# Staged weight forms, stores on another queue and moved cache copies in a hybrid decoder layer

## The chip, the cores and the metric

The kernel runs on one core of a Trainium2 chip. The metric is device time in microseconds (us) for one execution of the whole program, the median over several runs. A change of under 0.2% (about 4 us here) can't be told from none.

## The reference, cut to what matters

One decoder layer is computed for 1024 prompt positions and 8 single-token samples (1032 columns), D_MODEL 1024, all in float32:

```python
h = _rms_norm(x, g_mix_pre)
q, k, v, c_b, u, g_a, g_c = _project(h, w_in)      # u = c_c * c_h; w_in is 1024 x 9728
o, lse = ...                                       # attention in 3 head groups, dilations 1, 4, 16
kv_s = concatenate([cache, new k and v])[-n_past:] # cache rows moved by one
a = attn @ w_attn_o
c = (c_b * causal_conv(u, conv_w)) @ w_conv_o
mix = (sigmoid(g_a) * a + sigmoid(g_c) * c) @ w_o
x = x + _rms_norm(mix, g_mix_post)
x = x + _rms_norm(square(relu(_rms_norm(x, g_ffn_pre) @ w_ff1)) @ w_ff2, g_ffn_post)
```

The samples read caches of 128, 512 and 1024 rows; those caches, moved by one row, are outputs too, copied from DRAM to DRAM.

## The kernel before

Activations lie feature-major: 128 partitions by 1032 columns per feature tile. To keep float32 accuracy TensorE multiplies two rounded parts: every operand is a pair hi + lo, and each product is three matmuls (hi·hi, lo·hi, hi·lo). A weight tile of 128x512 arrives from DRAM as `wr` (issued on SP's queue, L169), `split` makes `wh` with a copy on ScalarE (L177) and `wl` with a subtraction on VectorE or GpSimd (L178). The pool holds five such pairs in the middle of the program (seven from the attention output projection on).

The program goes through these stages:

1. Norm, then per head the q, k, v projections beside the attention (to about 620 us). At the end of each of the eight heads `copy_piece(2)` issues two cache copies of up to 1 MB, of 57 in all, on ScalarE's queue (L334).
2. `tsums` (L965): sums of halves of h for a 2x2 Strassen-Winograd scheme: VectorE and GpSimd make T1, T2, T3, T4 in two halves (j = 0, 2), each split into hi and lo. Beside them TensorE does two plain gate tiles (`gate_raw`).
3. 17 *pairs* of weight columns. `strassen` (L1001) computes two 128-column results from seven products p0 to p6 of 24 matmuls each, accumulated in PSUM tiles A, B, C in the order B A C B A B C. The evictions are done by ScalarE and VectorE: after p1 `A` is copied (L1018) and `B` is added to it (L1019); only then may p3 write `B` again. The seven weight forms of a pair are sums of its four `wr` tiles (`s1`, `s2` and others), four of them made on GpSimd by `combine` (L133). "u" pairs give conv_C and conv_h (their product goes into E, then a three-tap convolution makes y, L1086 to L1089); "y" pairs give conv_B, multiplied with y (L1066); "g" pairs give gates. y and g results are stored to DRAM (`cv_d`, `g_d`) on GpSimd's queue (L1067). 15 pairs run in a pool `cw`, beside the samples' attention (`sample_steps`, advanced in two of five half products: loads `kt`, `qb` on SP's queue, products on GpSimd, sums on VectorE), and two gate pairs in a pool `pre`, beside the scaling and splitting of the attention output (`split_heads`: DMAs for `num` and `rden`, product L1119). After each pair of the 15 `copy_piece(2)` issues two more copies, after the last two pairs four.
4. The attention output projection "wao" with the gates as multipliers (`gr` from `g_d`, sigmoid L1167, product L1171, stored as `m2_d`); the conv output is loaded and split. Then "wco", "wo", and the squared-ReLU MLP ("wf1", "wf2").

The weights' work is issued ahead: `tick()` runs once per half product; if the form's raw tiles were requested two ticks ago and a `wh`/`wl` pair is free, `split_next` issues for the next form the GpSimd sum, the ScalarE copy and the VectorE subtraction at once. Each engine runs its instructions in order, so whatever stands behind such an instruction waits with it. `pin` keeps instructions in the order of the program; a scheduler places the others.

Of the kernel before, what the change touches and what calls it, by code (L numbers as in the profile page):

```python
# [13 lines left out]
OP = mybir.AluOpType  # L14
# [23 lines left out]
def tile_decoder_layer(  # L38
# [63 lines left out]
    todo = [(64, 65), (66, 67), (70, 71), (72, 73), (74, 75)]  # L102
# [6 lines left out]
    gate_pairs = todo  # L109
# [62 lines left out]
    def split(raw, space, eng, pin_):  # L172
# [5 lines left out]
        pin_(eng.tensor_tensor(lo, raw, hi.bitcast(F32), op=OP.subtract))  # L178
        return hi, lo, space

    def split_next():
# [4 lines left out]
        ready.append((key, split(form(rs), space, lo_eng[turn[0] % len(lo_eng)], lo_pin[0])))  # L186
        for j in free:
            raws.pop((plan_key, keys[j]))[2][2] += 1
# [5 lines left out]
    def tick():  # L194
        clock[0] += 1
        if forms and max(e[2] for e in spaces) > 0 and loaded(2):
            split_next()
        fetch()

    def take(key):  # L200
        while not ready:
            if loaded(0):
                split_next()
# [140 lines left out]
    with ExitStack() as st:  # L344
# [388 lines left out]
        for h in range(8):  # L733
# [24 lines left out]
            copy_piece(2)  # L758
# [194 lines left out]
    with tc.tile_pool(name="tsum", bufs=1) as ts:  # L953
# [5 lines left out]
        def tsums(j):  # L959
            js, ks = slice(j, j + 2), slice(4 + j, 6 + j)  # L960

            def new(name, bufs=1):
                return ts.tile([P, 2, HT], F32, name=name, bufs=bufs)

            def parts(eng, n, t):  # L965
                nc.scalar.copy(TS[n][0][:, js], t)
                eng.tensor_tensor(TS[n][1][:, js], t, f32(TS[n][0][:, js]), op=OP.subtract)
            b12, b22, T2, T3, T4 = new("b12", 2), new("b22", 2), new("T2", 2), new("T3"), new("T4")
            V, G, S = nc.vector.tensor_tensor, nc.gpsimd.tensor_tensor, OP.subtract
            V(b12, f32(hh[:, js, t2]), f32(hl[:, js, t2]), op=OP.add)  # L970
# [12 lines left out]
            yield  # L983
# [5 lines left out]
        for j in (0, 2):  # L989
            for _ in tsums(j):  # L990
                run(g, 2)
# [43 lines left out]
    with ExitStack() as st:  # L1035
# [15 lines left out]

        def drive(g):
# [8 lines left out]
        def stores(D, dst, ys=None):  # L1061
            def after(p):
                if p in DONE:
# [3 lines left out]
                    nc.gpsimd.dma_start(dst[a][:, t], D[a][:, t])  # L1067
            return after
        i, ys = 0, []
        for kind, *pair in pairs:  # L1070
            D1 = cw.tile([P, T], F32, name="D1")
            if kind == "u":
                E = cw.tile([P, 2 + T], F32, name="E", bufs=2)
                nc.gpsimd.memset(E[:, 0:2], 0.0)
                u = E[:, 2:]

# [4 lines left out]
                drive(strassen(pair, (D1, u), after))  # L1081
# [10 lines left out]
            else:  # L1092
                D = D1, cw.tile([P, T], F32, name="D2")
# [4 lines left out]
            copy_piece(2)  # L1098
# [6 lines left out]
    with tc.tile_pool(name="apool", bufs=1) as apool:  # L1105
        ah = apool.tile([P, 4, T], F32R, name="ah")
        al = apool.tile([P, 4, T], F32R, name="al")
        with tc.tile_pool(name="pre", bufs=1) as pre:
            def split_heads():
                for n in range(4):  # L1110
# [5 lines left out]
                    yield  # L1116
                    yield
                    yield
# [12 lines left out]
            for pair in gate_pairs:  # L1131
# [3 lines left out]
                for _ in strassen(pair, D, stores(D, [g_d[m - 60] for m in pair])):  # L1135
                    run(heads, 1)
            run(heads)
            copy_piece(4)
# [6 lines left out]
        with tc.tile_pool(name="cpool", bufs=1) as cpool:  # L1145
# [3 lines left out]
            with tc.tile_pool(name="sga", bufs=1) as sga:  # L1149
                cvs, grs = [], []  # L1150
# [13 lines left out]
                for i in range(KT):  # L1164
                    load_gate()
                    load_cv()
                    nc.scalar.activation(grs[i], grs[i], AF.Sigmoid)  # L1167
# [13 lines left out]
                    copy_piece(1)  # L1181
# [3 lines left out]
            with tc.tile_pool(name="sgc", bufs=1) as sgc:  # L1185
# [10 lines left out]
                for _ in range(3):  # L1196
                    load()
                nc.scalar.activation(got[0][0], got[0][0], AF.Sigmoid)
                for i in range(KT):
# [11 lines left out]
                    copy_piece(1)  # L1211
# [319 lines left out]
```

## Time and profile before

| | us |
|---|---|
| median of three runs (2123.06 to 2126.0) | 2124.21 |
| profiled execution | 2112.52 |
| its span (first to last instruction) | 2110.3 |
| TensorE busy in the span | 1971.2 (93%) |
| VectorE / ScalarE / GpSimd busy | 1236.2 / 733.1 / 601.2 |

The profiled execution is one run on its own and 11.7 us shorter than the median; sums over the profile are made against 2112.5. A busy TensorE isn't always at full speed: the granted clock is given beside it (1.00 is full). "Idle before ... <- X" names what ended an idle time.

### The profile page before, as it was taken

To read this page: it belongs to the slowest core of one execution; us is meant where nothing else is said; L and a number is where in the kernel's file an instruction comes from. 1 tells how busy PE (TensorE), PEld (TensorE's weight loads), DVE (VectorE), ACT (ScalarE), POOL (GpSimd) and SP (SyncE) were. 2 spreads that over 40 slices of the span, in tenths; PEclk is the share of its full clock that TensorE was granted. 3 is DMA by queue.
4 is the path that set the end of the run, shared out by engine and by line. 5 is a ranking of instruction groups with operands and counts; after the bars stand their busy time and mean duration, and the time that the engine had idled before them with its cause. 6 is when DMAs were issued, how large, how long until landed. Compare 5 with 4: busy or idle time off the path is not lost.

```text
span 2110.3 us, 33274 instructions
## 1 busy us (share of the span) xinstructions
PE 1971.2 (93%) x13253; PEld 1945.9 (92%) x13253; DVE 1236.2 (59%) x2081; ACT 733.1 (35%) x1448; POOL 601.2 (28%) x523
## 2 busy tenths in 40 slices
PE   7999999999996889888976999999999999999997
PEld 6999999999995889888976999999999999999996
DVE  7678777787646667485553441644554554444546
ACT  4355544554433213222233334453222221222233
POOL 3233332333237444444130223211111110101113
PEclk8999999999997889999988999999999999999998
DMA  4212122313231574554569542311111111111112
GB/s 141 57 64 77 50 72 66 103 43 98 91 115 61 197 248 168 201 178 158 186 190 374 184 133 78 94 51 40 51 40 51 51 43 49 51 41 50 51 31 81
DMA packets 84459, 216.74 MB, mean 103 GB/s; under 512 B 12000, under 2 KB 22368, under 8 KB 83408
## 3 DMA queue, kind: packets, MB, share of 16 engines
q1 hardware_dynamic: 65280, 112.77, 16.7%
q10 hardware_dynamic: 8112, 68.78, 9.4%
q0 software_dynamic: 10912, 33.06, 4.9%
q8 instruction: 104, 1.70, 0.3%
q14 instruction: 51, 0.42, 0.1%
HBM read 184.17 MB, written 84.86 MB: 127 GB/s over the span
## 4 chain that ended last, share of the span: by engine, by line
PE 48%; DVE 6%; DMA 6%; issue 4%; POOL 2%; ACT 1%; SPq 0%; ACTq 0%; DVEq 0%; POOLq 0%
PE ps_mm L218 14%; PE ps_mm L222 14%; PE ps_mm L221 14%; DVE wl L178 2%; DMA qb<-sq_d 1%; PE ps_b L1011 1%; PE ps_b L1015 1%; PE ps_b L1016 1%; DMA kt<-in_cache_dram 1%; DMA gr<-g_d 1%; POOL s L133 1%; DMA rden<-rden_d 1%; DMA g_d<-D 1%; DMA m_d<-gr 1%; PE ps_a L1011 1%
## 5 line engine op out<-in xcount | busy, mean ns | idle before, releaser
L178 POOL TENSOR_TENSOR wl<-wr,wh 128x512 fp32r<-128x512 f32 x152 | 201.8, 1328 | 803.6 <-ACT wh L177 703.2
L177 ACT CAST wh<-wr 128x512 fp32r<-128x512 f32 x320 | 193.3, 619 | 534.7 <-PE ps_mm L221 267.0
L218 PE MATMUL ps_mm<-hh,wh 128*128 128x344 f32 x1008 | 329.6, 327 | 2.5 <-ACT hh L307 1.9
L221 PE MATMUL ps_mm<-hl,wh 128*128 128x344 f32 x1008 | 324.2, 322 | 3.7 <-DVE hl L301 1.9
L222 PE MATMUL ps_mm<-hh,wl 128*128 128x344 f32 x1008 | 323.3, 321 | 0.0
L178 DVE TENSOR_TENSOR wl<-wr,wh 128x512 fp32r<-128x512 f32 x168 | 149.9, 894 | 173.9 <-ACT wh L177 173.8
L218 PE MATMUL ps_mm<-gh,wh 128*128 128x344 f32 x768 | 246.2, 321 | 0.0
L218 PE MATMUL ps_mm<-rh,wh 128*128 128x344 f32 x768 | 245.8, 320 | 0.0
L222 PE MATMUL ps_mm<-rh,wl 128*128 128x344 f32 x768 | 245.8, 320 | 0.0
L221 PE MATMUL ps_mm<-gl,wh 128*128 128x344 f32 x768 | 245.4, 319 | 0.0
L222 PE MATMUL ps_mm<-gh,wl 128*128 128x344 f32 x768 | 245.3, 319 | 0.0
L221 PE MATMUL ps_mm<-rl,wh 128*128 128x344 f32 x768 | 245.0, 319 | 0.0
L1368 DVE TENSOR_TENSOR f<-ps_mm,f 128x344 f32<-128x344 f32 x336 | 170.4, 514 | 110.2 <-PE ps_mm L222 109.6
L221 PEld LDWEIGHTS ps_mm<-hl,wh 128*128 128x128 f32 x1008 | 190.7, 189 | 5.7 <-DVE hl L301 3.2
L218 PEld LDWEIGHTS ps_mm<-hh,wh 128*128 128x128 f32 x1008 | 191.1, 190 | 3.9 <-ACT hh L307 2.9
L222 PEld LDWEIGHTS ps_mm<-hh,wl 128*128 128x128 f32 x1008 | 190.8, 189 | 0.0
L221 PEld LDWEIGHTS ps_mm<-gl,wh 128*128 128x128 f32 x768 | 144.8, 188 | 0.0
L222 PEld LDWEIGHTS ps_mm<-gh,wl 128*128 128x128 f32 x768 | 144.7, 188 | 0.0
L218 PEld LDWEIGHTS ps_mm<-gh,wh 128*128 128x128 f32 x768 | 144.7, 188 | 0.0
L218 PEld LDWEIGHTS ps_mm<-rh,wh 128*128 128x128 f32 x768 | 144.3, 188 | 0.0
L221 PEld LDWEIGHTS ps_mm<-rl,wh 128*128 128x128 f32 x768 | 144.3, 188 | 0.0
L222 PEld LDWEIGHTS ps_mm<-rh,wl 128*128 128x128 f32 x768 | 144.2, 188 | 0.0
(327 smaller groups left out, 4574.2 us busy)
## 6 DMA issues: line engine op xcount, KB each, us to landing
wr<-in_win_dram SPq DMA_DIRECT2D x152, 256.0 KB, 2.8
wr<-in_wf_dram SPq DMA_DIRECT2D x128, 256.0 KB, 2.8
out_okv_dram<-in_cache_dram ACTq DMA_DIRECT2D x16, 1020.0 KB, 8.2
kt<-in_cache_dram SPq DMA_DIRECT2D x32, 256.0 KB, 3.6
g_d<-D POOLq DMA_DIRECT2D x20, 258.0 KB, 3.2
x_sb<-in_xT_dram SPq DMA_DIRECT2D x12, 344.0 KB, 5.7
cv_d<-D POOLq DMA_DIRECT2D x16, 258.0 KB, 2.4
gr<-g_d POOLq DMA_DIRECT2D x8, 516.0 KB, 14.4
```

The lines of the kernel that those rows point to most:

```text
L133: pin(nc.gpsimd.tensor_tensor(out, x, y, op=op))
L177: pin_(nc.scalar.copy(hi, raw))
L178: pin_(eng.tensor_tensor(lo, raw, hi.bitcast(F32), op=OP.subtract))
L218: ins = nc.tensor.matmul(ps, wh, rh, start=(first and i == 0), stop=False)
L221: nc.tensor.matmul(ps, wh, rl, start=False, stop=False)
L222: nc.tensor.matmul(ps, wl, rh, start=False, stop=(last and i == n - 1))
L1011: ins = nc.tensor.matmul(acc[s], w[0][:, k], r[0][:, k], start=(p < 3 and k == 0), stop=False, skip_group_check=True)
L1015: nc.tensor.matmul(acc[s], w[0][:, k], r[1][:, k], start=False, stop=False, skip_group_check=True)
L1016: nc.tensor.matmul(acc[s], w[1][:, k], r[0][:, k], start=False, stop=(k == 3), skip_group_check=True)
L1368: pin(nc.vector.tensor_tensor(d, ps, d, op=OP.add))
```

## The change

- **Stages.** `split_next` becomes three functions. `stage_sum` issues the GpSimd sum, `stage_hi` at least two ticks later the ScalarE copy, `stage_lo` one tick after that the subtraction. Up to three sums may stand ready. Only pairs go this way.
- **Sums of h.** T3 moves from GpSimd to VectorE; both halves of `tsums` advance together, with T2 of both ahead of T3 and T4.
- **Tiles and stores.** u pairs alone use D1, y and g pairs have D2 and D3. u pairs' weights are swapped, E is one tile, cleared once. Stores of y and g results go out on SP's queue, three half products after the value is issued; in `pre` they stay on GpSimd's.
- **Order of pairs.** u g u y, twice, then u u y, twice (before: u u y g three times, then u u y); three gate pairs instead of two run in `pre`. `split_heads` leaves six half products instead of three between its loads and the product.
- **Copies.** Four per head under the attention (before two), none in stage 3 and under wao and wco; the 25 that are left go out in the MLP, where the program already had `copy_piece(2)`.
- **wao and wco.** The first gate tile is loaded and put through the sigmoid under the last gate pair (`gr0`); wco keeps two loaded chunks instead of three.

```diff
-        pairs += [("u", m, m + 1), ("u", m + 3, m + 4), ("y", m + 2, m + 5)]
-        if i < 6:
-            pairs.append(("g", *todo.pop(0)))
+        pairs.append(("u", m + 1, m))
+        if i < 4:
+            pairs.append(("g", *gate_pairs.pop(0)))
+        pairs += [("u", m + 4, m + 3), ("y", m + 2, m + 5)]
...
+    def stage_sum():
         plan_key, keys, key, _, form, free = forms.pop()
         rs = [raws.get((plan_key, k), (None,))[0] for k in keys]
+        summed.append((plan_key, keys, key, form(rs), free, clock[0]))
+
+    def stage_hi():
+        plan_key, keys, key, raw, free, _ = summed.pop(0)
         space = max(spaces, key=lambda e: e[2])
...
+        if plan_key[0] == "pair":
+            w, rest = split(raw, space, eng, lo_pin[0], True)
+            halves_.append((key, w, rest, done))
+        else:
+            ready.append((key, split(raw, space, eng, lo_pin[0])))
+            done()
+
+    def stage_lo():
+        key, w, rest, done = halves_.pop(0)
+        rest()
+        ready.append((key, w))
+        done()
...
     def tick():
         clock[0] += 1
-        if forms and max(e[2] for e in spaces) > 0 and loaded(2):
-            split_next()
+        if halves_:
+            stage_lo()
+        if summed and max(e[2] for e in spaces) > 0 and clock[0] > summed[0][5] + 1:
+            stage_hi()
+        if forms and len(summed) < 3:
+            one = forms[-1][0][0] == "one"
+            if (not one or (not summed and not halves_ and max(e[2] for e in spaces) > 0)) and loaded(2):
+                stage_sum()
+                if one:
+                    stage_hi()
         fetch()
...
-            copy_piece(2)
+            copy_piece(4)
...
             V(T2, b22, T1[:, js], op=S)
+            yield
             parts(nc.vector, 2, T2)
             yield
-            G(T3, b22, b12, op=S)
-            parts(nc.gpsimd, 3, T3)
             yield
+            T3, T4 = new("T3"), new("T4")
+            V(T3, b22, b12, op=S)
+            parts(nc.vector, 3, T3)
             G(T4, f32(hh[:, ks, t1]), T2, op=S)
...
-        for j in (0, 2):
-            for _ in tsums(j):
-                run(g, 2)
+        for _ in zip(tsums(0), tsums(2)):
+            run(g, 2)
...
+        def store(age):
+            while waiting and beat[0] - waiting[0][0] >= age:
+                _, dst, src = waiting.pop(0)
+                pin(nc.sync.dma_start(dst, src))
+
         def drive(g):
             for _ in g:
                 beat[0] += 1
+                store(3)
...
-                    nc.gpsimd.dma_start(dst[a][:, t], D[a][:, t])
+                    if later:
+                        waiting.append((beat[0], dst[a][:, t], D[a][:, t]))
+                    else:
+                        nc.gpsimd.dma_start(dst[a][:, t], D[a][:, t])
...
-                D = D1, cw.tile([P, T], F32, name="D2")
+                D = [cw.tile([P, T], F32, name=f"D{a}") for a in (2, 3)]
...
-            copy_piece(2)
+        store(0)
         run(steps)
...
-                    yield
-                    yield
-                    yield
+                    for _ in range(6):
+                        yield
                     nc.vector.tensor_tensor(ar, ar, rd, op=OP.mult)
...
                     raw_spaces.pop()
+                    nc.gpsimd.dma_start(gr0, g_d[8])
...
-            copy_piece(4)
+            nc.scalar.activation(gr0, gr0, AF.Sigmoid)
...
-                    copy_piece(1)
...
-                        gr, m2 = (sgc.tile([P, CH], F32, name=nm, bufs=3) for nm in ("grc", "m2c"))
+                        gr, m2 = (sgc.tile([P, CH], F32, name=nm, bufs=2) for nm in ("grc", "m2c"))
```

Three places show what moves on the engines; a number behind a name tells tiles of one name apart. First VectorE behind the attention, from the end of T2's sums to the splitting of T1 (`hl`). `b12`, `b22` are sums of parts of h, `t2l` and `t3l` the lo parts of T2 and T3, `s1`, `s2` sums of weights; before:

```order
L972 TENSOR_TENSOR T1_6725<-b12_6846,hh_95 128x1032
L973 TENSOR_TENSOR T1_6725<-T1_6725,hl_96 128x1032
L974 TENSOR_TENSOR T2_6848<-b22_6847,T1_6725 128x1032
L967 TENSOR_TENSOR t2l_6714<-T2_6728,t2h_6713 128x1032
L178 TENSOR_TENSOR wl_6757<-s2_6754,wh_6756 128x512
L178 TENSOR_TENSOR wl_6826<-wr_6568,wh_6825 128x512
L178 TENSOR_TENSOR wl_6842<-s1_6752,wh_6841 128x512
L967 TENSOR_TENSOR t2l_6714<-T2_6848,t2h_6713 128x1032
L178 TENSOR_TENSOR wl_6934<-wr_6542,wh_6933 128x512
L178 TENSOR_TENSOR wl_6952<-wr_6760,wh_6951 128x512
L996 TENSOR_TENSOR hl_96<-T1_6725,hh_95 128x2x516 x2
```

The same place of the changed kernel:

```order
L1006 TENSOR_TENSOR t2l_6730<-T2_6744,t2h_6729 128x1032
L1006 TENSOR_TENSOR t2l_6730<-T2_6752,t2h_6729 128x1032
L180 TENSOR_TENSOR wl_6811<-s2_6774,wh_6810 128x512
L180 TENSOR_TENSOR wl_6844<-wr_6582,wh_6843 128x512
L180 TENSOR_TENSOR wl_6860<-s1_6772,wh_6859 128x512
L1006 TENSOR_TENSOR t3l_6732<-T3_6863,t3h_6731 128x1032
L180 TENSOR_TENSOR wl_6950<-wr_6556,wh_6949 128x512
L1019 TENSOR_TENSOR T3_6872<-b22_6751,b12_6750 128x1032
L180 TENSOR_TENSOR wl_6967<-wr_6776,wh_6966 128x512
L1036 TENSOR_TENSOR hl_96<-T1_6741,hh_95 128x2x516
L1006 TENSOR_TENSOR t3l_6732<-T3_6872,t3h_6731 128x1032
L1036 TENSOR_TENSOR hl_96<-T1_6741,hh_95 128x2x516
```

The second `t2l` now stands ahead of the first weights, and T3 with `t3l` has come from GpSimd and stands between the weights and the two `hl`.

Second VectorE in a u pair, from the eviction behind p1 (L1019, later L1059) to that behind p3 (L1021 and L1022, later L1061 and L1062). `s_7120` and `s_7359` serve this pair's p5 or p6, `s_7434` and `s_7631` are the next pair's first sum; before, in the second pair:

```order
L1019 TENSOR_TENSOR D_7322<-ps_b,E 128x258 x2
L178 TENSOR_TENSOR wl<-s_7120,wh 128x512
L178 TENSOR_TENSOR wl<-s_7434,wh 128x512
L1021 TENSOR_TENSOR E<-ps_b,E 128x258
L1022 TENSOR_TENSOR E<-ps_c,E 128x258
L848 TENSOR_REDUCE ss<-kt 128x8
```

In the changed kernel, in the third pair, its second u pair:

```order
L1059 TENSOR_TENSOR E<-ps_b,D_7609 128x258
L180 TENSOR_TENSOR wl<-s_7359,wh 128x512
L887 TENSOR_REDUCE ss<-kt 67x8
L1061 TENSOR_TENSOR D_7609<-ps_b,D_7609 128x258
L1062 TENSOR_TENSOR D_7609<-ps_c,D_7609 128x258
L180 TENSOR_TENSOR wl<-s_7631,wh 128x512
```

The next pair's first `wl` now stands behind the first half of p3's eviction instead of ahead of it.

Third GpSimd in a y pair, the third of four in both kernels: stores (DMA `cv_d`), sums of weights (`s1`, `s2`, `wr`) and the samples' products (`kt`, `acc`); before:

```order
L899 TENSOR_TENSOR acc_9897<-kt_9800,ss_7249 128x512
L1067 DMA cv_d_61<-D2_9781 128x516
L899 TENSOR_TENSOR kt_9836<-kt_9836,ss_7249 128x512
L1067 DMA cv_d_61<-D1_9780 128x516
L899 TENSOR_TENSOR kt_9894<-kt_9894,ss_7249 67x512
L1067 DMA cv_d_61<-D2_9781 128x516
L133 TENSOR_TENSOR wr_9539<-wr_9579,wr_9539 128x512
L899 TENSOR_TENSOR acc_10032<-kt_9938,ss_7249 128x512
L1067 DMA cv_d_61<-D1_9780 128x516
```

In the changed kernel:

```order
L938 TENSOR_TENSOR kt_9827<-kt_9827,ss_7266 128x512
L938 TENSOR_TENSOR kt_9880<-kt_9880,ss_7266 67x512
L133 TENSOR_TENSOR s2_9789<-wr_9757,s2_9789 128x512
L938 TENSOR_TENSOR acc_10016<-kt_9923,ss_7266 128x512
L133 TENSOR_TENSOR s1_10063<-wr_9825,wr_10011 128x512
L133 TENSOR_TENSOR s2_10065<-s1_10063,wr_9862 128x512
L938 TENSOR_TENSOR kt_9973<-kt_9973,ss_7266 128x512
L938 TENSOR_TENSOR kt_10013<-kt_10013,ss_7266 67x512
L133 TENSOR_TENSOR wr_9825<-wr_9862,wr_9825 128x512
```

The four stores are gone from GpSimd's order; they stand on SP's queue between the loads of `wr` and `kt`.

## Rows read from the trace of the kernel before

**Rows 1.** Windows by stage: start:end, length, busy of PE, PEld, DVE, ACT, POOL, PEclk, DMA share, GB/s.

```profile
642.30:694.20 51.90, 31.30 (x208) 28.29 (x207) 27.68 (x38) 21.41 (x42) 39.90 (x35) 0.74 0.23 69
694.20:1001.80 307.60, 266.01 (x2043) 259.94 (x2042) 201.81 (x305) 77.83 (x160) 142.99 (x128) 0.93 0.57 194
...
1042.00:1100.40 58.40, 42.53 (x339) 41.93 (x338) 31.05 (x49) 19.57 (x33) 17.48 (x25) 0.88 0.60 185
1100.40:1171.00 70.60, 49.15 (x286) 48.03 (x285) 25.03 (x48) 21.47 (x32) 8.75 (x17) 0.85 0.93 340
```

**Rows 2.** The same view: single pairs (u, y, u) and a stretch of wco.

```profile
803.20:825.40 22.20, 20.60 (x171) 20.22 (x170) 20.07 (x33) 6.90 (x14) 13.10 (x10) 1.00 0.49 167
924.00:950.80 26.80, 22.80 (x174) 22.15 (x173) 23.53 (x30) 6.83 (x14) 14.92 (x14) 0.94 0.54 180
1001.80:1021.90 20.10, 20.10 (x170) 20.10 (x170) 13.09 (x24) 6.94 (x14) 1.29 (x1) 1.00 0.42 144
1200.00:1240.00 40.00, 40.00 (x256) 40.00 (x255) 18.14 (x37) 12.06 (x26) 10.18 (x19) 1.00 0.46 137
```

**Rows 3.** Waits, 642 to 1171 us: engine, line, releaser: us in total, times, longest.

```profile
DVE wl L178 <- ACT wh L177: 99.2, 34, 9.0
...
PE ps_b L1011 <- DVE D L1019: 46.6, 12, 13.0
POOL cv_d L1067 <- DVE D L1066: 45.7, 16, 8.4
POOL kt L843 <- DMA qb<-sq_d: 40.2, 8, 14.3
...
ACT gr L1167 <- DMA gr<-g_d: 34.2, 5, 12.6
...
PE ps_mm L218 <- DVE gr L1171: 21.5, 4, 12.7
...
DVE D L1019 <- DMA g_d<-D: 17.7, 3, 7.3
...
DVE num L1119 <- DMA rden<-rden_d: 15.6, 1, 15.6
```

**Rows 4.** Timeline of POOL, ACT and DVE in the second pair: start, us, [idle before <- releaser].

```profile
706.92 1.29 POOL L843 TENSOR_TENSOR kt<-kt,qb 128x512 f32<-128x512 f32 x1 [14.31 <-DMA qb<-sq_d]
...
710.81 0.62 ACT L177 CAST wh<-s 128x512 fp32r<-128x512 f32 x1 [9.65 <-POOL E L1074]
...
711.46 1.13 DVE L178 TENSOR_TENSOR wl<-s,wh 128x512 fp32r<-128x512 f32 x1 [9.00 <-ACT wh L177]
```

**Rows 5.** Timeline around the sums of h, from DVE, POOL, ACT and PE.

```profile
633.03 1.22 DVE L974 TENSOR_TENSOR T<-b,T 128x1032 f32<-128x1032 f32 x1
...
638.79 3.32 DVE L974 TENSOR_TENSOR T<-b,T 128x1032 f32<-128x1032 f32 x1
...
637.75 3.27 POOL L981 TENSOR_TENSOR T<-T,hl 128x1032 f32<-128x1032 f32 x1
...
642.68 1.05 ACT L966 CAST t2h<-T 128x1032 fp32r<-128x1032 f32 x1 [7.11 <-DMA den_d<-den_row]
...
658.19 0.58 PE L1015 MATMUL ps_b<-t2l,wh 128*128 128x258 f32 x1 [7.41 <-DVE t2l L967]
```

**Rows 6.** DMA issues in 694 to 1002 us: queue, count, KB each, median us to landing.

```profile
out_okv_dram<-in_cache_dram ACTq DMA_DIRECT2D x8, 1020.0 KB, 8.0
...
qb<-sq_d SPq DMA_DIRECT2D x15, 256.0 KB, 9.2
...
qb<-sq_d SPq DMA_DIRECT2D x8, 128.0 KB, 3.3
```

**Rows 7.** Landing of `wr` (L169): first line 30 to 600 us, second line 690 to 1000 us.

```profile
DMA to landing us min/median/max: 2.6/2.7/3.1
...
DMA to landing us min/median/max: 2.6/4.5/9.6
```

**Rows 8.** VectorE's subtraction in 694 to 1002 us, by shape: busy, mean ns.

```profile
L178 DVE TENSOR_TENSOR wl<-wr,wh 128x512 fp32r<-128x512 f32 x49 | 48.9, 1001 | 24.9 <-ACT wh L177 24.9
```

More of the change, by code (lines that the diff above doesn't have):

```diff
@@ L170, in fetch, with split @@
             raws[plan_key, (name, m, i)] = raw, clock[0], space
-    def split(raw, space, eng, pin_):
+    def split(raw, space, eng, pin_, later=False):
         pool, bufs = space[0:2]
@@ L177, in split, with rest, done @@
         pin_(nc.scalar.copy(hi, raw))
-        pin_(eng.tensor_tensor(lo, raw, hi.bitcast(F32), op=OP.subtract))
+        def rest():
+            pin_(eng.tensor_tensor(lo, raw, hi.bitcast(F32), op=OP.subtract))
+        if later:
+            return (hi, lo, space), rest
+        rest()
         return hi, lo, space
-    def split_next():
+    summed, halves_ = [], []
+    def stage_sum():
         plan_key, keys, key, _, form, free = forms.pop()
         rs = [raws.get((plan_key, k), (None,))[0] for k in keys]
+        summed.append((plan_key, keys, key, form(rs), free, clock[0]))
+    def stage_hi():
+        plan_key, keys, key, raw, free, _ = summed.pop(0)
         space = max(spaces, key=lambda e: e[2])
         turn[0] += 1
-        ready.append((key, split(form(rs), space, lo_eng[turn[0] % len(lo_eng)], lo_pin[0])))
-        for j in free:
-            raws.pop((plan_key, keys[j]))[2][2] += 1
+        eng = lo_eng[turn[0] % len(lo_eng)]
+        def done():
+            for j in free:
+                raws.pop((plan_key, keys[j]))[2][2] += 1
+        if plan_key[0] == "pair":
[6 more added lines that the diff above has]
+        key, w, rest, done = halves_.pop(0)
+        rest()
+        ready.append((key, w))
+        done()
     def loaded(age):
@@ L201, in take @@
         while not ready:
-            if loaded(0):
-                split_next()
+            if halves_:
+                stage_lo()
+            elif summed:
+                stage_hi()
+            elif loaded(0):
+                stage_sum()
             else:
@@ L967, in parts @@
                 eng.tensor_tensor(TS[n][1][:, js], t, f32(TS[n][0][:, js]), op=OP.subtract)
-            b12, b22, T2, T3, T4 = new("b12", 2), new("b22", 2), new("T2", 2), new("T3"), new("T4")
             V, G, S = nc.vector.tensor_tensor, nc.gpsimd.tensor_tensor, OP.subtract
+            b12, b22, T2 = new("b12", 2), new("b22", 2), new("T2", 2)
             V(b12, f32(hh[:, js, t2]), f32(hl[:, js, t2]), op=OP.add)
@@ L1059, in tile_decoder_layer, with stores @@
         DONE = {3: (1, t2), 4: (0, t1), 5: (1, t1), 6: (0, t2)}
-        def stores(D, dst, ys=None):
+        def stores(D, dst, ys=None, later=True):
             def after(p):
@@ L1066, in after @@
                         nc.vector.tensor_tensor(D[a][:, t], D[a][:, t], ys[a][:, t], op=OP.mult)
-                    nc.gpsimd.dma_start(dst[a][:, t], D[a][:, t])
-            return after
+                    if later:
+                        waiting.append((beat[0], dst[a][:, t], D[a][:, t]))
+                    else:
+                        nc.gpsimd.dma_start(dst[a][:, t], D[a][:, t])
+            return after
+        E = cw.tile([P, 2 + T], F32, name="E")
+        nc.vector.memset(E[:, 0:2], 0.0)
+        u = E[:, 2:]
         i, ys = 0, []
         for kind, *pair in pairs:
-            D1 = cw.tile([P, T], F32, name="D1")
             if kind == "u":
-                E = cw.tile([P, 2 + T], F32, name="E", bufs=2)
-                nc.gpsimd.memset(E[:, 0:2], 0.0)
-                u = E[:, 2:]
+                D1 = cw.tile([P, T], F32, name="D1")
                 def after(p):
@@ L1080, in after @@
                         nc.vector.tensor_tensor(u[:, t], u[:, t], D1[:, t], op=OP.mult)
-                drive(strassen(pair, (D1, u), after))
+                drive(strassen(pair, (u, D1), after))
                 nc.scalar.copy(up[:, i, :], E[:, NQ:NQ + 2])
@@ L1107, in tile_decoder_layer @@
         al = apool.tile([P, 4, T], F32R, name="al")
+        gr0 = apool.tile([P, T], F32, name="gr0")
         with tc.tile_pool(name="pre", bufs=1) as pre:
@@ L1134, in tile_decoder_layer @@
                     raw_spaces.pop()
-                for _ in strassen(pair, D, stores(D, [g_d[m - 60] for m in pair])):
+                    nc.gpsimd.dma_start(gr0, g_d[8])
+                for _ in strassen(pair, D, stores(D, [g_d[m - 60] for m in pair], None, False)):
                     run(heads, 1)
             run(heads)
-            copy_piece(4)
+            nc.scalar.activation(gr0, gr0, AF.Sigmoid)
         t_stack.close()
@@ L1166, in tile_decoder_layer @@
                     load_cv()
-                    nc.scalar.activation(grs[i], grs[i], AF.Sigmoid)
+                    if i:
+                        nc.scalar.activation(grs[i], grs[i], AF.Sigmoid)
                     def use_a(c, ps):
@@ L1195, in load @@
                         got.append((gr, m2))
-                for _ in range(3):
+                for _ in range(2):
                     load()
```

7 lines of the change are left out of this document (3 added, 4 removed).

## The prediction, made before the changed kernel was run

> **What bounds the kernel now.** I read the page's slices first. TensorE is 93% busy over the span, and what it loses lies between 640 and 1171 us: in the MLP behind it and the attention ahead of it hardly a wait is left. Then windows by stage. A pair that meets no obstacle takes 20.1 us at a granted clock of 1.00 [rows 2]. Against it the first pair takes 51.9 us, the next twelve 307.6 us (12 x 20.1 = 241.2), the last two 58.4 us (40.2) [rows 1]; two pairs between them run clean. The attention output projection has 288 matmuls; at wco's 40.0 us for 256 [rows 2] that is 45.0 us, and it takes 70.6 [rows 1]. So the excess is 31.8 + 66.4 + 18.2 + 25.6 = 142 us, part of it a low clock behind the waits (0.74, 0.93, 0.88, 0.85), and no gain from this change can be much larger.
>
> The waits say why. TensorE waits most for L1019, the addition that frees PSUM tile B for p3: 46.6 us in twelve waits [rows 3]. That addition is short; it is late because VectorE stands in front of it in a subtraction `wl` whose `wh` isn't there: 99.2 us [rows 3]. The timeline of the second pair shows the whole chain: GpSimd waits 14.31 us for the samples' `qb`, the sums of weights queued behind that product are late, ScalarE's copy waits 9.65 us, VectorE's subtraction 9.00 us, and the evictions stand behind it [rows 4]. Two lesser causes are values that can't be written because D1's or D2's last store hasn't landed (17.7 us for `g_d`), and GpSimd's stores, which wait 45.7 us for VectorE with sums of weights queued behind them [rows 3].
>
> **The change part by part.** All sums go by the profiled execution, 2112.5 us.
>
> *Sums of h and the first pair.* Before, VectorE's sums share their time with GpSimd's: the same T2 subtraction takes 1.22 us alone and 3.32 us beside GpSimd's 3.27 us [rows 5]. The first t2h starts at 642.68, behind `den_row`'s store, and that store stands behind T4's two instructions on GpSimd; order shows T4 still there, so I leave the first wait. What goes is the second t2l behind three weights (a wait of 7.41 us, [rows 5]) and GpSimd's T3. The new end is set by VectorE: from t2l to the second `hl`, which p2 needs, 13 instructions stand in its queue (12 of them shown). At 1.22 us each they end 16 us after 643.7, at 660; at 3.32 us each 43 us after it, at 687. GpSimd has T4 and four sums to do in that time, so part of them meets it: I take two thirds at the low figure, 1.9 us, 25 us, 669. Behind lie half of p2 and four products, 4.5 x 2.87 = 13 us: the pair ends at 682 instead of 694.2. Gain 12, bounds 21 and -6.
>
> *The twelve pairs (now fourteen less the first).* Staging puts at least two half products (2.9 us) between sum and `wh`, and one (1.4 us) between `wh` and `wl`. B is free in time if L1019 comes within about 3.5 us of its place (p2's 2.87 us and a half product, less the two evictions), so GpSimd may now be late by 2.9 + 1.4 + 3.5 = 7.8 us instead of 3.5 before TensorE notices. And it will be late less: the 24 stores of the twelve pairs leave its queue, with their waits. The copies leave too: a 256 KB `qb` lands in 9.2 us (128 KB: 3.3), beside copies that take 8.0 us each [rows 6], and `wr` lands in 4.5 us (up to 9.6) where it took 2.7 without them [rows 7]. With own tiles a y or g result waits for a store one or two pairs back, so the 17.7 us go. What is late next is VectorE itself. It is busy 201.8 us in the twelve pairs, 16.8 us per pair [rows 1], but a u pair with the samples' sums took 20.07 us of it and a y pair 23.53 [rows 2], as long as TensorE's own time or longer. Of the eleven pairs with samples' work, eight heavy ones should run near 21.5 us, the light ones at 20.1 to 20.5. I keep 16 us of excess and gain 50; bounds 66 (nothing left) and 20 (the heavy ones at 24 us, the others at 21). The reordered pairs change only where the heavy ones lie; a g pair moved to the next stage takes its 20.1 us with it.
>
> *Stores on SP's queue.* They are issued three half products, 4.3 us, behind the value. If it is later still, `wr` and `kt`/`qb` behind them wait too; `wr` has six buffers, four pairs of parts stand ready, 11 us of TensorE, so I price it at 0. If that cover is gone it is a rival below.
>
> *The gate pairs and the heads.* VectorE waited 15.6 us for `rden`, TensorE 13.0 us in the longest wait of its group [rows 3]. The product now stands six half products, 8.6 us, behind the loads' place. The loads start only when the tiles under them are free, one store's landing after the last y pair: I keep 5 us of 18.2, gain 13; bounds 18 and 0.
>
> *The attention output projection.* TensorE waits 21.5 us for products with the gate, ScalarE 34.2 us for `gr` [rows 3]. The first gate is now ready beforehand. The stage moved 340 GB/s for 70.6 us, 24.0 MB, at a DMA share of 0.93 [rows 1]; the seven copies in it go, 7.1 MB. The remaining 16.9 MB need 50 us at that rate, 5 us more than TensorE's 45. I keep 8 us of 25.6, gain 17; bounds 25 and 8. wco's prefetch of two chunks instead of three is hidden by the products that run meanwhile, 40.0 us of TensorE without a gap [rows 2]; uncovered it costs about one landing, 3 us by `qb`'s and `wr`'s [rows 6, 7].
>
> *The copies elsewhere.* Sixteen more in the attention are issued in ScalarE's slack, and `wr` there landed within 3.1 us with two copies per head [rows 7]; the 25 in the MLP meet a stage that needs weights seven pairs deep. I take -2 us together; bounds 0 and -8. Uncovered it is the last rival.
>
> The sum: 12 + 50 + 13 + 17 - 2 = 90, so 2022 us for an execution like the profiled one. The median of the runs is 11.7 us above it (2124.2 against 2112.5); I carry that over: **2034 us**.
>
> **The rivals.**
>
> 1. *VectorE becomes the bound of the pairs.* For it: 23.53 us in one y pair and 20.07 in one u pair [rows 2], subtractions of 1001 ns in the mean [rows 8], and T3 is added. Against it: those times hold what GpSimd's neighbours add, and GpSimd loses its stores. Then 45 us of excess stay in the pairs: 29 more than above, 2063 us. The Trainium skill (SBUF — State Buffer, SBUF: two separate sides) says that VectorE with two SBUF inputs and GpSimd reading SBUF lock one port pair for a whole instruction, and the other one is blocked. The trace agrees (1.22 against 3.32 us, rows 5); by that rule the work that stays on GpSimd goes on stretching VectorE, which is this rival.
> 2. *Nothing is left.* The chains are gone and slack suffices everywhere: gains of 21 + 66 + 18 + 25 and no cost, 130 us: 1994 us. For it: two pairs without samples' loads run at exactly 20.1 us, even with two copies each. Against it: those pairs had VectorE free.
> 3. *The queue of SP takes the place of GpSimd's.* A store that waits for VectorE holds `wr` and `qb`, as the products did before; the pairs gain nothing, only the other stages do: 2112.5 - 40 + 11.7 = 2084 us. That is also the case in which the change doesn't do what it says. For it: SP's order now has four stores per y or g pair between weights. Against it: 4.3 us of delay, and on GpSimd's queue the longest such wait was 8.4 us [rows 3]. The Trainium skill (DMA: Bandwidth & Descriptors, Issuing engines are not separate DMA queues) says that transfers of all issuing engines share the same 16 DMA engines and that another issuer saves only issue time. By that rule the move itself would give no bandwidth; no row of before shows stores on SP.
> 4. *Slower.* The copies under attention and MLP make weights late where TensorE has no wait now: if `wr` lands in 9.6 us as among the pairs [rows 7] and every one of the 8 + 13 groups of copies held ScalarE and then TensorE for the whole difference to 2.8, that is 21 x 6.8 = 143 us, 2177 us. It decides from 90 / 21 = 4.3 us per group. Against it: 3.1 us at most in the attention, with half as many copies.
>
> **How the numbers follow.** The forecast's own spread (2014 to 2054) 0.52; rival 1 0.20, rival 2 0.15, rival 3 0.08, rival 4 0.03; 0.02 is left for no change. The point is the likeliest case's. The range takes in the forecast, rival 1 to 2068 and the half of rival 2 that leaves a few us in each stage, from 2000: 0.8. Faster by over 0.2% (4 us): all but rival 4 and the rest, 0.95; same 0.02; slower 0.03.
>
> **What would show it.** In the changed profile: the wait of TensorE for the addition behind p1 well under 15 us in total instead of 46.6; VectorE's wait for `wh` under 40 us instead of 99.2; `qb` landing in 3 to 5 us; pairs between 20 and 22 us with a clock of 1.00; p3 of the first pair near 669 us; the wait for `rden` under 6 us; the output projection about 53 us long. Wrong it would be if VectorE stood over 95% busy in the pairs (rival 1), if SP's stores waited for VectorE while weights are late (rival 3), or if TensorE's waits appeared in the attention or the MLP (rival 4). An error in carrying over the 11.7 us would move the number without touching the reasons.

## The result, and the profile after

The changed kernel takes 2034.55 us in the median of four runs (2032.52 to 2038.89) against 2123.64 us before: a ratio of 0.9588 (95% interval 0.956 to 0.9616), 89 us less, and 0.6 us from the forecast. The profiled execution took 2032.5 us with a span of 2030.7. From profile to profile the gain is only 80 us, and a part of the point's accuracy is luck; both are taken apart below.

Windows by stage, of the changed kernel (columns as in [rows 1]): the first pair from the end of the plain gate tiles, the thirteen pairs behind it, the three gate pairs, these sixteen together, the output projection, and two pairs, the second a y pair:

```profile
642.30:689.90 47.60, 30.47 (x216) 27.84 (x215) 34.64 (x44) 21.10 (x42) 36.80 (x33) 0.82 0.27 86
689.90:963.70 273.80, 269.91 (x2210) 266.34 (x2210) 228.45 (x333) 88.39 (x177) 150.84 (x98) 0.99 0.40 126
963.70:1034.00 70.30, 63.64 (x506) 62.24 (x505) 42.02 (x65) 26.44 (x44) 23.47 (x32) 0.98 0.56 166
689.90:1034.00 344.10, 333.55 (x2713) 328.58 (x2713) 270.47 (x398) 114.82 (x221) 174.31 (x130) 0.99 0.43 134
1034.00:1085.70 51.70, 47.42 (x291) 46.89 (x290) 27.33 (x50) 21.18 (x33) 7.99 (x15) 0.97 0.79 282
854.30:875.80 21.50, 21.33 (x175) 20.69 (x174) 21.11 (x27) 7.93 (x16) 16.56 (x10) 1.00 0.34 111
875.80:901.30 25.50, 22.63 (x174) 21.99 (x173) 24.36 (x33) 7.83 (x16) 14.52 (x10) 0.93 0.31 99
```

The same sixteen pairs and projection of the kernel before, cut at the same products:

```profile
694.20:1100.20 406.00, 348.54 (x2714) 341.87 (x2713) 260.42 (x399) 110.70 (x219) 167.63 (x159) 0.93 0.57 190
1100.20:1171.50 71.30, 49.85 (x291) 48.73 (x290) 25.23 (x48) 21.50 (x32) 9.03 (x17) 0.86 0.93 339
```

Sixteen clean pairs are 321.6 us, so their *excess* fell from 84.4 to 22.5 us (below, each kernel's excess is such a window less 321.6). Of these 62 us, 47 are idle time of TensorE (406.0 less 348.5, against 344.1 less 333.6) and 15 are busy time that got shorter, as the clock rose from 0.93 to 0.99. In the projection the DMA share is 0.79 instead of 0.93.

The waits of the changed kernel, 642 to 1110 us, that answer to [rows 3]:

```profile
POOL kt L882 <- DMA qb<-sq_d: 15.4, 8, 5.2
DVE wl L180 <- ACT wh L177: 12.1, 6, 4.8
PE ps_tq L821 <- ACT kt L824: 10.9, 1, 10.9
DVE num L1170 <- DMA rden<-rden_d: 7.4, 2, 4.3
PE ps_b L1051 <- DVE D L1059: 7.0, 4, 2.9
```

The addition behind p1 (L1059) costs TensorE 7.0 us instead of 46.6, VectorE waits 12.1 us for `wh` instead of 99.2, GpSimd's stores to `cv_d` are gone. TensorE's longest wait, 10.9 us in the first pair, is one that the prediction didn't have; the kernel before has it too:

```profile
PE ps_tq L782 <- ACT kt L785: 7.0, 1, 7.0
```

### The profile page after: what moved, and what is told of

Its sections match the earlier page's. It is cut to its first block, busy times and chain, and to the rows that moved or that the text cites. A ratio compares the mean times of both kernels' runs of the same rounds, so it can differ in the third digit from the quotient of the medians.

```text
span 2030.7 us, 33252 instructions
## 1 busy us (share of the span) xinstructions
PE 1955.0 (96%) x13253; PEld 1932.2 (95%) x13253; DVE 1243.6 (61%) x2086; ACT 735.3 (36%) x1448; POOL 602.6 (30%) x487
## 5 line engine op out<-in xcount | busy, mean ns | idle before, releaser
L180 DVE TENSOR_TENSOR wl<-wr,wh 128x512 fp32r<-128x512 f32 x168 | 139.7, 832 | 152.8 <-ACT wh L177 152.4
```

## Experiments

Time is the median of the runs; ratio and interval are against the kernel before on the same chip. Excess (sixteen pairs behind the first), projection and span are those of one profiled execution.

| kernel | time | ratio | excess | projection |
|---|---|---|---|---|
| before | 2123.6 | | 84.4 | 71.3 |
| changed | 2034.6 | 0.9588 (0.956 to 0.9616) | 22.5 | 51.7 |
| changed, again (e12) | 2033.3 | 0.9603 (0.9582 to 0.9623) | 22.9 | 51.6 |
| e1 changed, no stages | 2045.4 | 0.9659 (0.963 to 0.9688) | 31.2 | 53.0 |
| e2 changed, copies back | 2071.6 | 0.9785 (0.976 to 0.9811) | 43.8 | 66.1 |
| e3 changed, stores on GpSimd's queue | 2031.9 | 0.9593 (0.9562 to 0.9623) | 28.5 | 52.8 |
| e4 changed, old order | 2034.5 | 0.9618 (0.9588 to 0.9649) | 25.5 | 56.4 |
| e5 before, stages alone | 2083.4 | 0.9822 (0.9791 to 0.9854) | 52.6 | 71.1 |
| e6 before, copies moved alone | 2071.5 | 0.9778 (0.9741 to 0.9814) | 55.2 | 50.7 |
| e7 before, stages and copies | 2042.4 | 0.9633 (0.9604 to 0.9662) | 29.1 | 54.6 |
| e8 changed, samples' steps later | 2031.5 | 0.9583 (0.9552 to 0.9615) | 22.3 | 52.8 |
| e9 e8 and `hl` first | 2033.8 | 0.9607 (0.9586 to 0.9628) | 24.7 | 49.3 |
| e10 changed, no stages, copies back | 2104.1 | 0.9932 (0.9911 to 0.9954) | 76.3 | 66.5 |
| e11 changed, no stages, stores on GpSimd's queue | 2055.4 | 0.9696 (0.9673 to 0.972) | 42.1 | 53.1 |

The profiled execution of the kernel before was 11 us faster than its median, those of e1, e6 and e11 were 5 to 8 us faster, those of e3, e4 and e10 were 6 to 8 us slower; a difference of excesses below 8 us means little there, and one between the two groups can be off by more.

**Undoing one part.** The question: is the slack of the stages what the pairs gained from, or the lighter traffic?

e1, where a form's sum, copy and subtraction are issued at once again:

```diff
-        if halves_:
-            stage_lo()
-        if summed and max(e[2] for e in spaces) > 0 and clock[0] > summed[0][5] + 1:
-            stage_hi()
...
+        if forms and max(e[2] for e in spaces) > 0 and loaded(2):
+            stage_sum()
+            stage_hi()
+            if halves_:
+                stage_lo()
```

> The changed kernel, but a pair's weight form is summed, copied and subtracted at one tick again; all else stays. Slack (my reasons): the stages are what lets TensorE ride over late sums, 7.8 us of tolerance against 3.5; without them 30 to 40 of the 62 us won in the pairs go back, VectorE waits over 60 us for wh again (12 now), TensorE over 25 us for the addition behind p1 (7 now), and the time is 2065 to 2075 us. Traffic (rival): the sums were late because copies and stores crowded the loads; these are gone, so one stage suffices, at most 10 us go back, and the time is 2037 to 2045 us.

Only 8.7 us of the pairs' 62 go back (11 us by the medians), 2045.4 us, the upper end of what "traffic" gave: "slack" as the main cause fell. The sixteen pairs of e1 (windows) and its waits, 642 to 1180 us (L1054 is the addition behind p1 here, L1056 the first eviction behind p3):

```profile
688.00:1040.80 352.80, 335.63 (x2715) 330.25 (x2714) 264.40 (x400) 114.15 (x221) 164.80 (x131) 0.99 0.42 132
```

```profile
DVE wl L180 <- ACT wh L177: 71.1, 33, 4.7
PE ps_b L1046 <- DVE D L1056: 9.8, 7, 2.3
PE ps_b L1046 <- DVE D L1054: 4.6, 3, 2.0
```

VectorE waits 71 us for `wh`, as expected of missing stages, and TensorE hardly notices: 4.6 us at the addition, and 1.6 more where it writes E; over 25 were expected. A large wait on an engine beside the bottleneck isn't yet a cost.

e2, the copies in their old places:

```diff
-            copy_piece(4)
+            copy_piece(2)
...
+            copy_piece(2)
         store(0)
```

and `copy_piece(4)` behind the gate pairs, `copy_piece(1)` per column tile of wao. The call in wco isn't put back; 50 of the 57 copies go out ahead of wao and seven in it, so there was none left for it.

> The changed kernel with the cache copies where they were (two per head, two per pair, four behind the gate pairs, one per column tile in wao and wco); stages, stores and order as changed. Slack: the stages swallow the later loads; the pairs lose 5 to 15 us, the output projection 8 to 12 of its 19, the tail gets 2 to 6 back: 2045 to 2055 us. Traffic: the pairs lose 35 to 45 us and the projection all of its 19, 2080 to 2095 us.

Between the two: the pairs lose 21 us, the projection 14.4. The loads are late as before; landing of `wr`, 690 to 1000 us, in e2:

```profile
DMA to landing us min/median/max: 2.7/5.1/10.8
```

e3, stores at once on GpSimd's queue (`later=False` for all pairs):

> The changed kernel with the stores of y and g results on GpSimd's queue at once, tiles D2 and D3 kept. My reasons: GpSimd waits 30 to 45 us for VectorE at these stores again with sums behind it, which with stages costs the pairs 5 to 10 us: 2040 to 2045 us. Rival (SP's queue only takes GpSimd's place): no difference or a gain, 2030 to 2036 us.

The time is the rival's; the wait that I expected came, its price can't be seen in the time. Waits of e3:

```profile
POOL cv_d L1118 <- DVE D L1114: 43.2, 15, 11.9
DVE wl L180 <- ACT wh L177: 12.2, 6, 4.6
```

GpSimd stands 43 us at the stores again, as expected, and VectorE's wait for `wh` stays at 12 us: the stages cover it. The pairs' excess is 6 us larger, in an execution 6 us slower than the median; the end of the program gives 4.4 us back (last section). The times can't tell e3 from the changed kernel.

e4, the old order of pairs (two gate pairs behind):

> The changed kernel with the old order of pairs (u u y g three times, then u u y; two gate pairs behind). My reasons: the order changes only where the heavy pairs lie; within 5 us of the changed kernel, 2030 to 2039 us, the third gate pair's wait moves with it. Rival (the order spreads VectorE's load and so is what removes the waits): the pairs lose 10 us or more, over 2044 us.

2034.5 us, and 25.5 us of excess in an execution 8 us slower than that: the order is worth nothing that these runs can measure.

**One part alone on the kernel before.** Undoing each part gave back 8.7, 21 and 6 us, 36 of the 62 us together. Either the parts cover for each other, or what wasn't undone (own tiles, the heads' six half products) holds the rest.

e5 (the three functions and `tick` of the change), e6 (the copies' lines of the change), e7 (both):

> The kernel before with the three stages alone; copies, stores, tiles, order and sums of h stay. The pairs' excess over 20.1 us each was 84 us before and is 23 us now, and undoing a single part gave back 9 us (stages), 21 us (copies), 6 us (stores). Overlap (either the slack or the lighter traffic hides most of the same waits): the stages alone take 30 to 45 us off, 2073 to 2090 us on a chip where before takes 2118. Addition (each part has its own waits, worth what its undoing cost): the stages alone take 5 to 12 us off, 2106 to 2113 us.

> The kernel before with the copies alone moved (four per head, none from the pairs to wco, the rest in the MLP). Overlap: the pairs give 35 to 50 us and the projection 13 to 16, the tail takes 3 to 6: 2060 to 2072 us where before takes 2118. Addition: the pairs give 18 to 24 us, 2083 to 2090 us.

> The kernel before with stages and moved copies; stores, shared tiles, order, sums of h, the heads' three half products and the gates as before. Overlap: these two are nearly all of it; the pairs' excess is 30 to 38 us (84 before), the first pair stays at 47 us, the projection at 55 to 60: 2043 to 2055 us. If own tiles and SP's queue matter more than their undoing showed, the excess stays over 45 us and the time over 2060 us.

In their times e5 and e6 came out by "overlap"; e7 lies just under its ranges (0.6 us in the time). The other parts were sized less well: e6 gave 29 us in the pairs (35 to 50 expected) and 20.6 in the projection (13 to 16) and lost nothing behind it (3 to 6). The stages alone take 32 us off the excess, the copies alone 29 (and 20.6 off the projection), both 55; by the medians 38, 50 and 79 us of the whole time. The sixteen pairs of e5 and of e6 (windows):

```profile
695.50:1069.70 374.20, 339.35 (x2715) 334.03 (x2715) 270.59 (x397) 112.69 (x219) 180.15 (x159) 0.96 0.61 205
```

```profile
695.40:1072.20 376.80, 341.88 (x2715) 336.31 (x2713) 262.30 (x399) 112.88 (x221) 171.36 (x159) 0.96 0.37 123
```

Waits of e5, 642 to 1180 us:

```profile
PE ps_b L1050 <- DVE D L1058: 34.7, 12, 11.8
DVE num L1158 <- DMA rden<-rden_d: 16.9, 1, 16.9
DVE D L1058 <- DMA g_d<-D: 14.6, 2, 8.3
DVE D L1058 <- DMA cv_d<-D: 12.1, 2, 8.3
DVE wl L180 <- ACT wh L177: 11.5, 4, 5.4
```

and of e6:

```profile
DVE wl L178 <- ACT wh L177: 80.8, 37, 8.9
PE ps_b L1011 <- DVE D L1019: 17.3, 7, 4.8
...
POOL kt L843 <- DMA qb<-sq_d: 5.2, 2, 4.7
```

The two cut different links. The stages remove VectorE's wait for `wh` (99.2 to 11.5) and leave the addition behind p1 late for other reasons: in five of TensorE's twelve waits (14.4 us) a shared tile's store hadn't landed for the addition or for ScalarE's copy ahead of it, and one (11.8 us) stands behind the product in the gate pairs that waits for `rden`. The copies leave VectorE waiting 80.8 us for `wh`, and TensorE's waits for the addition fall all the same, from 46.6 to 17.3 us: GpSimd waits 5.2 us for `qb` instead of 40.2, VectorE waits 13.1 us at the addition for stores of shared tiles instead of 26.6, and the gate pairs have no wait for it over 0.6 us. In e7 VectorE still waits 24 us for stores of shared tiles, and TensorE only 9.0 for the addition.

**The missing corners.** e10 (e1 and e2 together) and e11 (e1 and e3 together):

> The changed kernel without stages and with the copies in their old places: what stores, tiles and order do alone among the copies. With the copies moved the pairs' excess behind the first was 55 us with neither, 29 with stages, 31 with stores, tiles and order, 23 with both; among the copies it is 84 with neither, 52 with stages, 44 with both. Substitutes (stages and stores take away the same lateness): 55 to 65 us of excess, 2082 to 2092 us. If stores, tiles and order only help where the copies are gone: 75 to 84 us, 2100 to 2110 us.

> The changed kernel without stages and with the stores on GpSimd's queue; own tiles, order and moved copies stay. If SP's queue is the substitute for the stages, the pairs' excess goes from 31 us (without stages alone) back to 45 to 55 us, 2058 to 2070 us. If the own tiles and the order are, it stays at 31 to 37 us, 2045 to 2052 us.

e10 took the second way, 2104.1 us; its sixteen pairs (windows):

```profile
694.30:1092.20 397.90, 348.84 (x2715) 343.27 (x2714) 255.15 (x400) 113.17 (x221) 158.81 (x131) 0.93 0.57 191
```

By its excess that is 8 us less than before, by the medians 16 us less of the whole time. Two of its waits:

```profile
DVE wl L180 <- ACT wh L177: 100.8, 35, 11.1
POOL kt L877 <- DMA qb<-sq_d: 60.5, 14, 15.3
```

GpSimd stands behind late `qb` loads for 60.5 us (40.2 before). That it only reaches this wait sooner, having no stores in its queue, is a reading that no run tests. In e11 the pairs (windows) and the stores' wait are:

```profile
689.00:1052.70 363.70, 337.91 (x2714) 332.80 (x2713) 264.07 (x400) 113.73 (x221) 173.01 (x155) 0.98 0.40 128
```

```profile
POOL cv_d L1113 <- DVE D L1109: 45.9, 16, 15.4
```

This decides for neither side alone: own tiles, order and the rest bring the excess from 55.2 (e6) to 42.1, SP's queue from 42.1 to 31.2 (e1). By medians SP's queue is worth 10 us there (2055.4 to 2045.4; 8 by the ratios, whose intervals overlap), and nothing measurable with stages (e3). The Trainium skill (DMA: Bandwidth & Descriptors, Issuing engines are not separate DMA queues) says that another issuing engine only saves the time of issuing. Nothing in the trace speaks for bandwidth either: the DMA share is 0.40 in e11 and 0.42 in e1. What SP's queue takes away is GpSimd's wait of 45.9 us for VectorE, with sums of weights behind it.

The excess as a table:

| | copies in the pairs | copies moved |
|---|---|---|
| neither stages nor stores, tiles, order | 84.4 | 55.2 |
| stores, tiles, order (and the rest) | 76.3 | 31.2 |
| stages | 52.6 | 29.1 |
| both | 43.8 | 22.5 |

With copies moved, stages and stores are substitutes in part: 26 and 24 us alone, 33 together. With the copies in place they add up by this table (32 and 8, together 41), but the 84.4 and the 76.3 come from a fast and a slow execution; by the medians it is 38 and 16, together 46, so the contrast between the columns isn't shown. Moving the copies helps in every row, by 21 to 45 us.

**The first pair.** e8 starts the samples' steps later:

```diff
-                if beat[0] % 5 in (1, 3) or short[0]:
+                if beat[0] > 6 and (beat[0] % 5 in (1, 3) or short[0]):
```

> The changed kernel with the samples' steps started behind the sixth half product instead of the first. In the first pair TensorE stands 10.9 us at the samples' transposes, which wait for ScalarE's writes into tiles of a pool whose space comes free with the last of the sums of h (667.2 us). If that queue order is the cause, p1's second half runs in the gap, p2 starts at 667 to 668 instead of 672.8, and the first pair is 35 to 38 us long instead of 41.7; 2 to 6 us faster than the changed kernel. If the last hl is the real bound and the transposes only stand in front of it, the gap stays at p2 with 9 to 10 us and the time changes by under 2 us.

e9 besides puts both `hl` ahead of T3's second half on VectorE (`pin` on `hl` and T3, the second half's last part of `tsums` run behind `hl`):

> The changed kernel with the samples' steps later, and with both hl ahead of T3's second half and its lo part on VectorE. With the steps later p2 still waited 7.1 us for hl, which stood behind T3 (3.39 us) and t3l (1.22 us). If VectorE's order is the bound of the first pair, p2 starts 3 to 5 us earlier and the pair is 32 to 35 us long (41.7 in the changed kernel, 37.6 with later steps), 4 to 9 us less than the changed kernel in all. If VectorE's work as a whole is the bound, the wait moves to p3 behind t3l, the pair stays at 37 to 38 us, and the time is that with later steps alone, 1 to 4 us less.

The timeline of the first pair in the changed kernel (start, us, engine; from VectorE's, ScalarE's and TensorE's rows):

```profile
663.99 3.17 DVE L1036 TENSOR_TENSOR hl<-T,hh 128x1032 fp32r<-128x1032 f32 x1
...
667.23 0.34 ACTq L1078 DMA_DIRECT2D cwt<-in_convw_dram  x1
...
668.11 0.37 ACT L823 ACTIVATE kt<-ps_tq 8x256 f32<-8x256 f32 x1 [4.16 <-issue]
...
668.79 1.87 PE L821 MATMUL ps_tq<-ident,qks 128*8 128x128 f32 x8 [10.91 <-ACT kt L824]
670.31 0.56 PE L1051 MATMUL ps_a<-hh,wh 128*128 128x258 f32 x1
...
676.48 0.37 PE L1051 MATMUL ps_b<-t3h,wh 128*128 128x258 f32 x1
```

The samples' transposes stand in TensorE's queue inside p1 (`ps_a`) and wait for ScalarE's `kt`. Ahead of `kt` ScalarE's queue loads `cwt` (L1078), the first tile of the pool that takes the space of the sums of h; it goes out at 667.23, when the last `hl` ends. That this space is what ScalarE waits for is read from the program, the row names no releaser. So at 667.2 us half of p1 and all of p2 are still to do. With the steps later (e8) TensorE waits at p2 for `hl` instead:

```profile
661.63 0.58 PE L1055 MATMUL ps_c<-hl,wh 128*128 128x258 f32 x1 [4.46 <-DVE hl L1036]
666.09 0.58 PE L1055 MATMUL ps_c<-hl,wh 128*128 128x258 f32 x1 [2.63 <-DVE hl L1036]
```

The pair is 37.6 us long instead of 41.7 (counted from its first product), as the first alternative has it; the 7.1 us at `hl` are nearer to the second's 9 to 10. With the transposes out of the way `hl` is the next bound. The median, 2031.5 us with a ratio of 0.9583 (0.9552 to 0.9615), can't be told from the changed kernel's. e9 went neither way: 42.9 us, 2033.8 us (0.9607, 0.9586 to 0.9628). Its rows on VectorE and TensorE:

```profile
656.75 3.38 DVE L1039 TENSOR_TENSOR hl<-T,hh 128x1032 fp32r<-128x1032 f32 x1
...
661.20 3.40 DVE L1039 TENSOR_TENSOR hl<-T,hh 128x1032 fp32r<-128x1032 f32 x1
...
668.45 2.29 DVE L1006 TENSOR_TENSOR t3l<-T,t3h 128x1032 fp32r<-128x1032 f32 x1
...
673.14 0.58 PE L1055 MATMUL ps_b<-t3h,wh 128*128 128x258 f32 x1 [4.46 <-DVE E L1063]
```

`hl` came earlier on the queue but ran beside GpSimd's T4 and took 3.4 us twice (one of the two took 1.22 in the changed kernel); the last sum ended at 670.7 instead of 667.2, and p1's eviction, which needs a tile in that same space, held p3. The end of the last sum is the bound there, and `hl` in front only makes another sum the last; what GpSimd's share in it costs wasn't tried by itself. The Trainium skill (SBUF — State Buffer, SBUF: two separate sides) says that a VectorE instruction with two SBUF inputs and a GpSimd instruction that reads SBUF block each other for a whole instruction; the trace agrees, 3.4 against 1.22 us.

**The changed kernel again.**

> The changed kernel itself, as the measure for the other three on the same chip, and for the step from the profiled execution to the median: the kernel before ran 11.7 us longer in its median than in the execution that was profiled, the changed one 2.0 us. If that distance belongs to the one execution that happened to be profiled, the median is again 2030 to 2039 us and the profiled execution anywhere between its fastest and its slowest run, 2028 to 2041 us. If a profiled execution is systematically shorter, it lies 8 to 14 us below the median.

2033.3 us, its profiled execution 2033.0, excess 22.9 us: the first alternative.

## Why the prediction came out right, point by point

**Fourteen pairs and gate pairs** (50 + 13 = 63 us forecast): 62 measured. Here the signs held: 7.0 us for the addition behind p1 (under 15 forecast), 12.1 for `wh` (under 40), the thirteen pairs at 21.1 us each with a clock of 0.99, 12.5 us of excess in them (16 forecast in other pairs). The landing of `qb` isn't given in this trace; GpSimd's wait for it fell from 40.2 to 15.4 us. The gate pairs kept 10 us instead of 5, with waits for `rden` and `num` (7.4 us for `rden`, forecast under 6).

The size held, the order of causes didn't. The prediction put TensorE's 46.6 us at the addition down to VectorE standing in `wl`, and called stores of shared tiles a lesser cause. Rows of the kernel before, from VectorE and TensorE:

```profile
712.98 0.58 PE L1011 MATMUL ps_b<-t4h,wh 128*128 128x258 f32 x1 [4.26 <-DVE E L1021]
...
788.67 0.76 DVE L1019 TENSOR_TENSOR D<-ps_b,E 128x258 f32<-128x258 f32 x2 [4.14 <-DMA g_d<-D]
789.15 0.58 PE L1011 MATMUL ps_b<-t3h,wh 128*128 128x258 f32 x1 [5.04 <-DVE D L1019]
...
1061.58 1.23 DVE L1119 TENSOR_TENSOR num<-num,rden 128x1024 f32<-128x1024 f32 x1 [15.56 <-DMA rden<-rden_d]
1063.80 0.58 PE L1011 MATMUL ps_b<-t3h,wh 128*128 128x258 f32 x1 [13.02 <-DVE D L1019]
```

Taken one by one, the twelve waits are: six (20.2 us) where the addition itself waits for the store of a shared tile, two (15.7 us) behind the heads' products in the gate pairs, three (6.7 us) where VectorE is busy without a gap, and one (3.9 us) behind a `wl` that waits for `wh`. In the second pair the chain of [rows 4] ends in the eviction behind p3 (L1021) and costs 4.3 us there; the addition had run at 701.1, ahead of it. What made the stores land late isn't split up further. So VectorE's 99.2 us at `wh` reached TensorE directly in a small part of its waits; e1 has 71 us of them at a price of 8.7. That the stages alone still take 32 us off shows that lateness also travels on, along paths that these rows don't separate. The traffic of the copies alone is worth about as much.

In the gate pairs it was the copies and not the six half products. In the four kernels with the copies in place (before, e2, e5, e10; e2 and e10 with six half products) one wait behind the heads' product holds 11.8 to 15.0 us; in the ten without, e6 with three half products among them, no wait for the addition is over 4.8 us.

**The output projection** (17 forecast): 19.6, at 51.7 us (53 forecast). The copies make nearly all of it: e6, with nothing else changed, has 50.7 us. That 53 was so close is partly luck: the stage moves 14.6 MB (282 GB/s for 51.7 us) where the forecast left 16.9 (the four copies issued behind the gate pairs had run in it too), and it moves them at 282 instead of 340 GB/s: two errors that cancelled.

**First pair** (12 forecast): 4.3. This is the term that failed. The sums were sized well, the second `hl` ends at 667.2 (669 forecast); wrong was "behind lie half of p2 and four products". The samples' transposes held half of p1 as well, and p1's rest and p2 ran from 668.8 to 676.5, the first 4 us of it at a clock of 0.54. e8 takes 4 us of it back. The trace of before had shown the transposes' wait (7.0 us), and the sum left it out.

**Copies elsewhere** (-2): the place was wrong. The attention shows at most 1 us (first product of the pairs at 648.2 us, before at 647.1) and the MLP none: e6, whose copies alone were moved, spends 939.5 us behind the projection, and the kernel before 938.8. The changed kernel spends 945.0, and 4.5 us of these are the end of the program (below).

**The sum and the median.** 90 us were forecast from profile to profile; 4 + 62 + 20 - 6 = 80 came. The carried 11.7 us should have been about 2: the changed kernel's profiled executions lie 2.0 and 0.3 us below their medians, while the kernel before scattered from 2109.2 to 2126.0 us over the chips used here, and the one profiled (2112.5) was near its lower end. Ten us too much gain and ten us too much carried over cancelled. What scatters in the kernel before wasn't tried.

**The rivals.** VectorE as the bound shows in single pairs: its sign, over 95% busy, holds in three of the thirteen (19.9 of 20.5 us in the pair from 730.5 us, 21.11 of 21.50, and 24.36 of 25.50 in the y pair at 875.8 us), and only the last of them is more than 1.5 us over the clean 20.1; over the thirteen VectorE is busy 228.45 of 273.80 us. "SP's queue takes the place" is out: the pairs gained 62 us with it, and without stages the move itself looks like a gain (e11 against e1). "Nothing left" missed by the 22.5 us of the pairs and the first pair. "Slower" is out by e6's 939.5 us.

## What to carry to other kernels

Big copies that nobody waits for still cost whoever loads beside them; move them to the stage with the fewest waits before anything else. Between a late producer and the bottleneck, several links can be cut, and cutting one hides what the others are worth: undo each part, but also try each alone. A long wait on a side engine says only where lateness passes through; what it costs is read at the bottleneck, wait by wait, by looking at what stood last in front of each.

## What was not expected of the hardware

The time from VectorE's last instruction to the end of the span was 9.6 to 10.0 us in all eight kernels whose y and g stores stand on SP's queue (changed, e1, e2, e4, e8, e9, e10, e12) and 5.0 to 5.6 us in the six with these stores on GpSimd's queue (before, e3, e5, e6, e7, e11). VectorE's last row in the changed kernel (its span ends at 2030.7), and what SP's queue waits for from 2000 us on (L1565 is the end of the program, PEq TensorE's queue):

```profile
2019.29 1.41 DVE L1461 TENSOR_TENSOR f<-f,x 128x688 f32<-128x688 f32 x1
```

```profile
SPq L1565 <- PEq L1565: 5.7, 2, 5.2
SPq L1565 <- DMA out_yT_dram<-f: 2.8, 1, 2.8
```

and of e3 (2036.2):

```profile
2029.23 1.41 DVE L1461 TENSOR_TENSOR f<-f,x 128x688 f32<-128x688 f32 x1
```

```profile
SPq L1565 <- DMA out_yT_dram<-f: 3.1, 1, 3.1
SPq L1565 <- PEq L1565: 0.7, 2, 0.5
```

The same instructions issue the same stores, SP's queue waits 2.8 and 3.1 us for them to land, and in the changed kernel the end comes 4.4 us later. The difference is the closing wait for TensorE's queue: 5.6 to 5.7 us in all eight kernels, 0.6 to 1.0 in all six. Why some two dozen stores more on SP's queue, a thousand us earlier, lengthen it stays open; with the stages it takes back about what that queue gains.
